# Re-pricing the instructions of a two-block layer for the list schedule that orders them

## The chip, the cores and the metric

The kernel runs on one NeuronCore of one Trainium2 chip. The metric is the device time of one execution in microseconds (us); the slowest core counts, and here there is only one.

## The reference

Two transformer blocks run one after the other on 512 tokens of width 1024, in float32.

```python
def reference(x, ...):
    x = first_block(x, ...)    # hybrid_layer
    return second_block(x, ...)
...
def hybrid_layer(...):
    h = rms_norm(x, norm_pre_w); proj = h @ w_in
    moba_out = moba_attention(a_q, a_k, a_v) * silu(a_z)          # 8 heads of 64
    qkv = silu(causal_depthwise_conv([d_q, d_k, d_v], conv_w))
    o = gated_delta_rule(...)                                     # 4 heads of 128, chunks of 64
    mixed = concat(moba_out, rms_norm(o) * silu(d_z)) @ w_out
    return x + rms_norm(mixed, norm_post_w)
...
def second_block(...):
    y_a = hgrn2_mixer(...)        # 4 heads of 128, gated linear recurrence
    y_b = nsa_mixer(...)          # 8 heads of 64: compressed, selected and window attention
    merged = g_a * (y_a @ w_br_a) + g_b * (y_b @ w_br_b)
    h = x + merged @ w_out
    h = h + square(relu(rmsnorm(h) @ w_ff1)) @ w_ff2
    return rmsnorm(h, final_g)
```

The gated delta rule solves a unit lower triangular system for every head and chunk. HGRN2 masks a product of decayed queries and keys with a causal mask, head by head and tile by tile.

## The kernel before

**An order written by a planner.** The body does not issue instructions. Every call goes to a `Recorder`, which keeps operations with their engine, a price from `cost` in ns and their dependencies from the regions that they read and write. At the end `issue` runs a list schedule: `schedule` simulates five queues (TensorE, VectorE, ScalarE, GpSimd, the DMA issues of SyncE) with these prices, and with a hand-over time between engines from `delay` and the table `HOP`. At each step the engine that is free first takes the ready operation with the best rank. The rank comes from a schedule made backwards from the end, and the forward and backward passes are repeated four times; the order with the shortest planned end is issued. So a price changes no instruction: it changes the place of instructions in the queue of each engine. On the chip each queue runs in that fixed order, and an instruction waits for its inputs there.

All instructions are issued by one line of `issue`, line 274, so every row of the profile shows L274; the tile names tell them apart. `bank` is PSUM, `arena` a large SBUF area of many small tiles, `w_raw`, `w_hi` and `w_lo` weights before and after `split`, `ha`, `hb` and `kr` activations kept as pairs, `sp` small per-row numbers.

**Matrix products.** Each dense product is three TensorE products of split operands: `split` rounds 128x1024 weights on ScalarE (`w_hi`) and takes the rest on VectorE (`w_lo`). A unit is a weight load of 512 KB; two `w_raw` buffers and three of each part are in turn.

**The stages around the change.** The first block mixes, in `ORDER1`, for four delta rule heads `gdn_keys`, `gdn_inverse`, `gdn_states`, `gdn_finish`, the convolutions, and for four pairs of attention heads `moba_proj` and `moba_pair`. `gdn_keys` ends in `block_inverses`: 32 diagonal 16x16 blocks of all chunks lie on 32 partitions, and VectorE multiplies them out there by `tensor_tensor` over 4-dimensional views (4x4x4 and 8x8x8 elements, called block products here) and `tensor_reduce`; ScalarE transposes the result into `XT`, and DMAs carry it through DRAM (`blocks_x`) to the tile that TensorE reads in `gdn_inverse`. `moba_proj` empties PSUM by half partitions: `evq` through `halves`, and `evk`, in 64x512 instructions on ScalarE and VectorE. In the second block `ORDER2` mixes projections, `compress` (adds over `N_CMP` = 31 blocks), `hgrn_gates`, `hgrn_head` (two `copy_predicated` of 64 partitions per tile) and `hgrn_finish`, and then four `nsa_pair` follow. `rstd` and `rstd_of` take a power on GpSimd with `OP.pow`. The rest of the second block is dense products.

Of the kernel before, what the change touches and what calls it, by code (L numbers as in the profile page):

```python
# [30 lines left out]
OP = mybir.AluOpType  # L31
# [12 lines left out]
class Recorder:  # L44
# [5 lines left out]

    ENGINES = ("tensor", "vector", "scalar", "gpsimd", "sync")
    HOP = {("tensor", "vector"): 197, ("tensor", "scalar"): 197, ("tensor", "gpsimd"): 224,
           ("scalar", "scalar"): 148, ("scalar", "vector"): 142, ("scalar", "tensor"): 227,
           ("scalar", "gpsimd"): 170, ("gpsimd", "gpsimd"): 100, ("vector", "vector"): 127, ("vector", "scalar"): 150,
           ("vector", "tensor"): 220, ("vector", "gpsimd"): 155, ("gpsimd", "vector"): 60,
           ("gpsimd", "scalar"): 80, ("gpsimd", "tensor"): 150, ("tensor", "tensor"): 0}
    TABLE = {AF.Exp: 0, AF.Tanh: 0, AF.Ln: 1, AF.Sin: 2}

    def __init__(self, nc):
# [81 lines left out]
    def cost(self, name, method, args, kw):  # L141
        size = lambda a: int(np.prod([x[1] for x in list(a.ap)[1:]])) if len(a.ap) > 1 else 1
        psum = lambda a: isinstance(a, bass.AP) and a.space == PSUM
        n = size(args[0])
        scalars = 61.0 * sum(isinstance(a, bass.AP) for a in args[2:4])
        if method == "dma_start":
            return 475.0
        if name == "tensor":
            if args[1].dtype == F32R:
                return max(n / 2.4 + 13.0, 112.0)  # L150
            if method == "transpose":
                return 110.0
            return max(n / 1.2, 107.0) + max(n, size(args[1])) / 1.2 + 4.0
        if name == "scalar":
            scaled = any(isinstance(kw.get(k), bass.AP) for k in ("scale", "bias"))
            return n / 1.2 + (51.0 if psum(args[1]) else 94.0) + 93.0 * ("accum_out" in kw) + 93.0 * scaled
        if name == "vector":
            if method == "reciprocal":
                return 6.25 * n + 69.0
            if method == "tensor_reduce":  # L160
                n = size(args[1])
            if method == "tensor_tensor_scan":
                n *= 2
            if method == "tensor_tensor":
                return n / 0.96 + 69.0
            if method == "tensor_scalar":
                return n / (0.96 if psum(args[1]) else 1.92) + 69.0 + scalars
            if method == "scalar_tensor_tensor":
                return n / 0.96 + 69.0 + 61.0 * isinstance(args[2], bass.AP)
            two = method == "tensor_copy" and not psum(args[1])  # L170
            return n / (1.92 if two else 0.96) + 67.0
        if method == "tensor_tensor":
            return n * 165.0 + 300.0 if args[3] == OP.pow else n * 2.1 + 100.0
        return n + 70.0

    def transfer(self, out, src):
# [12 lines left out]
    def delay(self, i, k):  # L189

        a, b = self.ops[i], self.ops[k]
        if a.transfer:
            return 100.0
        if a.engine == b.engine and not b.deps[i]:
            return 0.0
        return self.HOP.get((a.engine, b.engine), 100.0)

    def schedule(self, order, before, after):
# [88 lines left out]
N_CMP = 31  # L287
# [1323 lines left out]
```

## Time and profile before

| what | value |
|---|---|
| median of 3 runs | 1114.79 us (1114.76 to 1116.5) |
| profiled execution | 1114.45 us, with a span of 1112.7 us from its first to its last instruction |
| TensorE busy | 1088.8 us, 98% of the span |
| VectorE, ScalarE, GpSimd busy | 781.4, 582.0, 41.1 us |

Busy time of TensorE is made of records whose ends are modelled and which overlap; its idle time is where no record lies. VectorE and ScalarE records also overlap a little with the next one of their queue, so the distance from start to start is shorter than a record where nothing is waited for.

### The profile page before, as it was taken

The numbers are of one execution on the slowest core, as the hardware profiler recorded it, in microseconds if no ns is written. First come the engines' busy times: TensorE is split into PE (matmuls) and PEld (weight loads), VectorE is DVE, ScalarE is ACT, GpSimd is POOL, SyncE is SP. The second block draws the span as 40 slices with busy tenths as digits, with TensorE's granted clock in tenths as the row PEclk, the third lists the DMA queues.
The fourth block names the chain that finished last, engine by engine and source line by source line (L and its number), as shares of the span: only waits on it lengthen the run. The fifth ranks groups of instructions, "written<-read, shape, count | busy, mean of one in ns | idle before, by whom it ended". The sixth has DMA issues, their size and how long they took to land. (4 is left out here: it accounts for less than half of the span.)

```text
span 1112.7 us, 15240 instructions
## 1 busy us (share of the span) xinstructions
PE 1088.8 (98%) x5712; PEld 901.3 (81%) x5712; DVE 781.4 (70%) x1607; ACT 582.0 (52%) x1059; POOL 41.1 (4%) x65
## 2 busy tenths in 40 slices
PE   8999999999999999999999999999999999999997
PEld 7887888787879877888777778888988888888885
DVE  7585877979666446688967654466678578488486
ACT  4655645574455534547765543345553553553564
POOL 1010101001000000000000000000000000000001
PEclk9999999999999999999999999999999999999999
DMA  5323122222542222224201163253205205205102
GB/s 214 133 87 97 50 82 82 79 61 85 177 145 87 102 84 70 67 96 142 96 20 58 44 240 112 96 167 112 102 19 187 97 19 198 105 1 208 38 1 77
DMA packets 44283, 109.60 MB, mean 99 GB/s; under 512 B 10416, under 2 KB 17968, under 8 KB 44208
## 3 DMA queue, kind: packets, MB, share of 16 engines
q1 hardware_dynamic: 44208, 108.62, 28.2%
q8 instruction: 45, 0.74, 0.3%
q14 instruction: 30, 0.25, 0.1%
HBM read 104.67 MB, written 3.93 MB: 98 GB/s over the span
## 5 line engine op out<-in xcount | busy, mean ns | idle before, releaser
L274 PE MATMUL bank<-ha,w_hi 128*128 128x512 f32 (+1 forms) x1504 | 460.7, 384 | 0.0
L274 PEld LDWEIGHTS bank<-ha,w_hi 128*128 128x128 f32 x1504 | 273.0, 189 | 46.2 <-issue 0.8
L274 PE MATMUL bank<-ha,w_lo 128*128 128x512 f32 (+1 forms) x752 | 287.0, 382 | 0.0
L274 DVE TENSOR_TENSOR w_lo<-w_raw,w_hi 128x1024 fp32r<-128x1024 f32 (+2 forms) x106 | 128.0, 1208 | 102.6 <-ACT w_hi L274 101.5
L274 ACT ACTIVATE w_hi<-w_raw 128x1024 fp32r<-128x1024 f32 (+2 forms) x106 | 110.9, 1047 | 153.8 <-PE bank L274 134.2
L274 DVE TENSOR_TENSOR w_lo<-arena,w_hi 128x1024 fp32r<-128x1024 f32 (+2 forms) x94 | 114.0, 1217 | 69.2 <-ACT w_hi L274 68.8
L274 ACT ACTIVATE w_hi<-arena 128x1024 fp32r<-128x1024 f32 (+3 forms) x102 | 102.5, 1005 | 114.9 <-PE bank L274 110.0
L274 PEld LDWEIGHTS bank<-ha,w_lo 128*128 128x128 f32 x752 | 141.8, 189 | 23.2 <-issue 0.3
L274 PE MATMUL bank<-w_hi,hb 128*128 128x512 f32 x416 | 133.6, 393 | 0.3 <-DVE x L274 0.3
L274 ACT ACTIVATE arena<-bank 128x512 f32<-128x512 f32 (+5 forms) x158 | 74.0, 484 | 60.5 <-PE bank L274 57.2
L274 PE MATMUL bank<-w_hi,ha 128*128 128x512 f32 (+3 forms) x384 | 98.1, 343 | 2.1 <-ACT w_hi L274 2.1
L274 ACT ACTIVATE arena<-arena,sp 128x384 f32<-128x384 f32 (+3 forms) x156 | 83.2, 560 | 31.8 <-DVE sp L274 28.0
L274 PE MATMUL bank<-arena 128*128 128x128 f32 (+9 forms) x672 | 96.6, 311 | 1.8 <-DVE arena L274 0.9
L274 PEld LDWEIGHTS bank<-arena 128*128 128x128 f32 (+2 forms) x672 | 76.8, 173 | 21.8 <-issue 12.3
L274 PEld LDWEIGHTS bank<-w_hi,hb 128*128 128x128 f32 x416 | 78.1, 188 | 16.8 <-DVE x L274 0.7
L274 PE MATMUL bank<-ident,arena 128*128 128x128 f32 (+1 forms) x476 | 83.4, 277 | 5.1 <-DVE arena L274 3.4
L274 PE MATMUL bank<-w_lo,hb 128*128 128x512 f32 x208 | 81.6, 392 | 0.4 <-DVE w_lo L274 0.4
L274 PEld LDWEIGHTS bank<-ident,arena 128*128 128x128 f32 (+1 forms) x476 | 58.6, 139 | 25.3 <-DVE arena L274 8.8
L274 PEld LDWEIGHTS bank<-w_hi,ha 128*128 128x128 f32 x384 | 67.0, 191 | 9.8 <-ACT w_hi L274 2.3
L274 PE MATMUL bank<-kr,hb 128*128 128x512 f32 (+3 forms) x288 | 71.3, 352 | 1.9 <-DVE sp L274 1.9
L274 DVE TENSOR_TENSOR arena<-arena 128x1024 f32<-128x1024 f32 (+9 forms) x136 | 69.3, 532 | 3.2 <-ACT arena L274 1.4
L274 POOL TENSOR_TENSOR sp<-sp,mhalf 128x1 f32<-128x1 f32 (+1 forms) x36 | 31.1, 863 | 999.6 <-DVE sp L274 994.9
(161 smaller groups left out, 1371.1 us busy)
## 6 DMA issues: line engine op xcount, KB each, us to landing
w_raw<-in_w_in_dram SPq DMA_DIRECT2D x62, 512.0 KB, 3.3
arena<-in_w_ff_dram SPq DMA_DIRECT2D x43, 512.0 KB, 4.3
w_raw<-in_w_ff_dram SPq DMA_DIRECT2D x21, 512.0 KB, 3.4
w_raw<-in_w_out_dram SPq DMA_DIRECT2D x17, 512.0 KB, 3.4
arena<-in_w_out_dram SPq DMA_DIRECT2D x9, 512.0 KB, 3.5
x<-in_x_dram SPq DMA_DIRECT2D x8, 512.0 KB, 5.6
arena<-in_w_in_dram SPq DMA_DIRECT2D x8, 512.0 KB, 3.2
arena<-blocks_x SPq DMA_DIRECT2D x8, 256.0 KB, 2.9
```

The lines of the kernel that those rows point to most:

```text
L274: self.issued.append((i, getattr(getattr(self.nc, ops[i].engine), method)(*args, **kw)))
```

## The change

The prices of `cost`, the hand-over table and `delay` take other values. No operation is added, removed or resized, and the order of calls in the body stays. All that can differ in the program is the order in which the planner puts them out.

```diff
     HOP = {("tensor", "vector"): 197, ("tensor", "scalar"): 197, ("tensor", "gpsimd"): 224,
-           ("scalar", "scalar"): 148, ("scalar", "vector"): 142, ("scalar", "tensor"): 227,
-           ("scalar", "gpsimd"): 170, ("gpsimd", "gpsimd"): 100, ("vector", "vector"): 127, ("vector", "scalar"): 150,
-           ("vector", "tensor"): 220, ("vector", "gpsimd"): 155, ("gpsimd", "vector"): 60,
-           ("gpsimd", "scalar"): 80, ("gpsimd", "tensor"): 150, ("tensor", "tensor"): 0}
+           ("scalar", "scalar"): 148, ("scalar", "vector"): 142, ("scalar", "tensor"): 250,
+           ("scalar", "gpsimd"): 271, ("gpsimd", "gpsimd"): 100, ("vector", "vector"): 127, ("vector", "scalar"): 150,
+           ("vector", "tensor"): 240, ("vector", "gpsimd"): 165, ("gpsimd", "vector"): 125,
+           ("gpsimd", "scalar"): 118, ("gpsimd", "tensor"): 150, ("tensor", "tensor"): 0}
...
-        n = size(args[0])
+        ap = list(args[0].ap)
+        n, half, small_ = size(args[0]), ap[0][1] == 64, 0.0
+        if name in ("vector", "scalar") and n >= 256 and half and psum(args[1]):
+            small_ = 100.0
+        if name == "vector" and len(ap) > 3 and ap[-1][1] <= 8:
+            small_ += 40.0 + (340.0 if n == 512 else 0.0)
...
-            return n / 1.2 + (51.0 if psum(args[1]) else 94.0) + 93.0 * ("accum_out" in kw) + 93.0 * scaled
+            if ap[0][1] == 32 and len(ap) > 2:
+                small_ = 240.0
+            return small_ + n / 1.2 + (51.0 if psum(args[1]) else 94.0) + 93.0 * ("accum_out" in kw) + 93.0 * scaled
...
             if method == "tensor_tensor":
-                return n / 0.96 + 69.0
+                return small_ + n / 0.96 + 69.0 + (105.0 if ap[-1][1] == N_CMP else 0.0)
+            if method == "copy_predicated":
+                return 302.0
...
             if method == "scalar_tensor_tensor":
-                return n / 0.96 + 69.0 + 61.0 * isinstance(args[2], bass.AP)
+                return small_ + n / 0.96 + 69.0 + 61.0 * isinstance(args[2], bass.AP)
...
         if method == "tensor_tensor":
-            return n * 165.0 + 300.0 if args[3] == OP.pow else n * 2.1 + 100.0
+            return n * 211.0 + 345.0 if args[3] == OP.pow else n * 2.1 + 100.0
...
         if a.engine == b.engine and not b.deps[i]:
-            return 0.0
+            return 0.0 if a.engine == "tensor" else 120.0
```

The last hunk is `delay`: a dependency inside one engine's queue where the later operation overwrites what the earlier one read or wrote, without reading it.

## Rows read from the trace of the kernel before

**Rows 1.** The page's busy time, share of the span and instructions by engine.
```profile
span 1112.7 us, 15240 instructions
PE 1088.8 (98%) x5712; PEld 901.3 (81%) x5712; DVE 781.4 (70%) x1607; ACT 582.0 (52%) x1059; POOL 41.1 (4%) x65
```

**Rows 2.** Windows by stage: length, then busy time by engine, TensorE clock, DMA share.
```profile
0.00:20.00 20.00, 15.20 (x93) 13.94 (x94) 12.67 (x28) 8.84 (x17) 3.42 (x12) 0.91 0.82 298
...
80.00:320.00 240.00, 235.27 (x1353) 192.67 (x1352) 184.07 (x421) 138.67 (x303) 17.42 (x21) 1.00 0.30 98
...
400.00:560.00 160.00, 154.35 (x870) 127.74 (x870) 126.72 (x399) 91.03 (x196) 6.79 (x10) 1.00 0.27 90
...
760.00:1100.00 340.00, 340.00 (x1582) 284.82 (x1581) 245.28 (x301) 169.59 (x213) 3.12 (x4) 1.00 0.24 86
1100.00:1112.70 12.70, 4.68 (x21) 3.52 (x19) 7.56 (x14) 4.12 (x10) 1.10 (x2) 0.79 0.38 143
```

**Rows 3.** Windows of 20 us: a dense one, and the one with most TensorE idle.
```profile
380.00:400.00 20.00, 20.00 (x90) 16.57 (x89) 4.90 (x4) 6.14 (x8) 0.00 (x0) 1.00 0.26 91
...
540.00:560.00 20.00, 18.18 (x117) 14.06 (x116) 19.87 (x76) 17.24 (x51) 0.00 (x0) 1.00 0.15 53
```

**Rows 4.** The waits of TensorE, 80 to 320 us: total, times, longest (us).
```profile
PE bank L274 <- DVE sp L274: 1.9, 2, 1.4
PE bank L274 <- DVE arena L274: 1.7, 4, 0.9
PE bank L274 <- DMA arena<-blocks_x: 0.7, 1, 0.7
```

**Rows 5.** The same for 400 to 560 us.
```profile
PE bank L274 <- DVE arena L274: 3.4, 7, 1.0
```

**Rows 6.** Timeline before the longest wait: start, us, what, [idle before].
```profile
130.85 1.04 DVE L274 TENSOR_TENSOR arena<-arena 32x512 f32<-32x512 f32 x1
...
134.07 1.19 DVE L274 TENSOR_TENSOR arena<-arena 32x512 f32<-32x512 f32 x1
...
137.35 0.50 PE L274 MATMUL bank<-kr,hb 128*128 128x512 f32 x1 [1.42 <-DVE sp L274]
```

**Rows 7.** Timeline, 86 to 204 us: half-partition evacuations back to back.
```profile
88.91 2.40 ACT L274 ACTIVATE kr<-bank 64x512 fp32r<-64x512 f32 x4
...
198.38 2.78 DVE L274 TENSOR_TENSOR kr<-bank,kr 64x512 fp32r<-64x512 f32 x4
```

**Rows 8.** Groups by shape, whole span: count | busy us, mean ns | idle before.
```profile
L274 PE MATMUL bank<-ha,w_lo 128*128 128x512 f32 x656 | 259.8, 396 | 0.0
...
L274 DVE TENSOR_TENSOR x<-x,bank 128x512 f32<-128x512 f32 x72 | 46.2, 678 | 4.7 <-PE bank L274 4.7
...
L274 DVE TENSOR_TENSOR kr<-bank,kr 64x512 fp32r<-64x512 f32 x16 | 11.0, 687 | 1.7 <-ACT kr L274 1.4
...
L274 DVE TENSOR_TENSOR arena<-arena 32x512 f32<-32x512 f32 x8 | 8.7, 1092 | 0.1
...
L274 POOL TENSOR_TENSOR sp<-sp,mhalf 128x4 f32<-128x4 f32 x16 | 19.1, 1192 | 373.3 <-DVE sp L274 373.2
```

**Rows 9.** Timeline, 415 to 437 us: a hand-over to TensorE, a power and its wait.
```profile
416.53 0.42 DVE L274 TENSOR_TENSOR kr<-bank,kr 128x256 fp32r<-128x256 f32 x1
...
417.00 0.44 PE L274 MATMUL bank<-ident,arena 128*128 128x128 f32 x2 [0.71 <-DVE kr L274]
...
433.61 1.92 POOL L274 TENSOR_TENSOR sp<-sp,mhalf 128x4 f32<-128x4 f32 x1 [85.80 <-DVE sp L274]
...
436.40 0.63 PE L274 MATMUL bank<-ident,arena 128*128 128x128 f32 x4 [0.79 <-DVE arena L274]
```

**Rows 10.** Timeline, 494 to 496 us: copies by mask and a wait.
```profile
494.98 0.54 DVE L274 COPY_PREDICATED arena<-hmask,bank 64x128 f32<-64x128 int32 x2
...
495.57 0.33 PE L274 MATMUL bank<-ident,arena 128*128 128x128 f32 x1 [0.40 <-DVE arena L274]
```

**Rows 11.** Timeline at 316 us: a weight split that TensorE waits for.
```profile
316.66 0.51 PE L274 MATMUL bank<-w_lo,hb 128*128 128x512 f32 x1 [0.44 <-DVE w_lo L274]
```

## The prediction

> **What bounds the kernel now.** I read the page's busy shares first. TensorE is busy 1088.8 of 1112.7 us; the next engine, VectorE, 781.4 [rows 1]. The change alters no instruction, so TensorE's work stays, and only its idle 23.9 us can grow or shrink. The second view, the windows by stage, says where that lies [rows 2]: 4.8 us in the first 20 us (loads of the input, and a clock of 0.91 there), 4.7 us between 80 and 320 (the first block's mixers), 5.7 us between 400 and 560 (the second block's), none from 760 to 1100, and 8.0 us in the last window, where TensorE has finished and the last norm and stores run. That leaves 23.9 - 4.8 - 4.7 - 5.7 - 8.0 = 0.7 us elsewhere. So the reorderable part is about 11.1 us in the middle; head and tail are chains of few operations.
>
> Idle time understates a wait. In a dense window TensorE starts 90 products in 20.00 us, one every 0.22 us [rows 3], while the record of one is 0.396 us long [rows 8]. A record thus covers 0.396 - 0.222 = 0.17 us in which nothing new starts, and a wait of 0.4 us costs nearly 0.6.
>
> The third view, TensorE's waits, says what ended them: in 80 to 320 us VectorE's `sp` and `arena` and the landing of `blocks_x`, 1.9 + 1.7 + 0.7 = 4.3 us in 7 waits [rows 4]; in 400 to 560 us VectorE's `arena`, 3.4 us in 7 waits [rows 5]. These are results that came later than the order had counted on.
>
> **The change, price by price.** An operation that the planner thinks too cheap finishes late on the chip, and its consumer then stands at the head of TensorE's queue with other ready products behind it. I compare old and new price with rows. A record of a plain VectorE evacuation is 678 ns [rows 8] and its price 512/0.96 + 69 = 602, so records exceed the time that the queue is held by some 76 ns.
>
> - Block products 32x512: record 1092 less 76 is about 1016; old price 602, new 982. Eight of them, 0.38 each; sixteen small ones get 0.04 each. The transposing ScalarE copy behind them gets 0.24. One head's chain was underpriced by 2 x 0.38 + 4 x 0.04 + 0.24 = 1.16 us. The longest wait of TensorE, 1.42 us, follows two of these products within 7 us [rows 6].
> - Half-partition evacuations: four on VectorE take 2.78 us, (2.78 - 0.687)/3 = 0.698 from start to start; four on ScalarE 2.40 us, about 0.60 [rows 7, 8]. Old prices 602 and 512/1.2 + 51 = 478, new 702 and 578. There are 32 on VectorE and 44 on ScalarE, 0.1 each, and they stand between the block products in the same queue.
> - Copies by mask: two of 64x128 last 0.54 us [rows 10]; the spacing is then about 0.3. Old price 128/0.96 + 67 = 200 (134 for the narrow one), new 302. For a tile's pair that is 0.27 us more. The adds over `N_CMP` blocks in the same stage get 0.105 each, sixteen of them.
> - Powers of four columns: mean record 1192 ns [rows 8]; old 960, new 1189. But one of 1.92 us is among them, and TensorE waited 0.79 us after it [rows 9]. The new price covers 0.23 of the 0.96 us by which that one ran over.
> - Hand-overs. VectorE to TensorE, 220 to 240: the evacuation that starts at 416.53 is priced 336, and TensorE starts at 417.00 [rows 9], 0.13 after its priced end. Both values are longer, the new one by 0.02 more; the order gets a little more slack. GpSimd to its readers gains 0.04 to 0.07. The 120 for overwriting inside one queue has no row that shows it. If the chip takes nothing there, the planner puts another operation into a hole of at most 0.12; if it takes 0.12, the same is saved. I count all hand-overs as nothing, with both signs open, because they work on VectorE and ScalarE, busy 70% and 52% [rows 1].
>
> In all VectorE's prices grow by 8 x 0.38 + 16 x 0.04 + 32 x 0.1 + 16 x 0.27 + 16 x 0.105 = 12.9 us, 1.7% of its work, nearly all of it in the two stages where TensorE waits.
>
> Against the ScalarE half-partition price speaks the Trainium skill, page "Perfetto Trace Analysis", section "Optimizing Scalar/DVE Operations": profiled latency is about twice the overhead that occupies the engine, and that overhead is some 51 ns for ScalarE on PSUM, which by my estimate gives 478, the old price. The spacing of 0.60 in the row disagrees, and the measurement decides; by the page, the new price would be 0.1 us too long for each of the 44, and the gain below would be smaller by at most 0.4 us.
>
> **The sum.** Of the 4.3 us in the first block [rows 4] I take all but 0.3, which stands behind a slow power: 4.0. In the second, four of the seven waits come straight behind copies by mask or those adds, of which [rows 10] shows one; I take a third of 3.4 us, 1.1 [rows 5]. Two slow powers give 2 x 0.23 = 0.5. Ten waits hide 0.17 each, 1.7. Together 7.3 us can be reached by right prices. The planner must find other ready products to fill with, and it moves everything, so new waits appear. Bounds of that share are nothing and all. I take 60%, because the dense windows show that weight products are there to fill with, while in 540 to 560 us VectorE itself is busy 19.87 of 20 us [rows 3] and nothing can be moved off it. That is 4.4 us. The profiled execution of 1114.45 us becomes 1110.1; the median lies 0.34 higher, so 1110.4.
>
> Head and tail I price at nothing. They run one chain: row sums, power, scaling, store. Their small powers go from 465 to 556 but have no other work to trade places with; a swap of two tiles there would cost or save about one 0.7 us operation.
>
> **Rivals.**
> - *The waits only move* (same). The mixers' chains are serial, and TensorE waits at another link. For it: VectorE at 19.87 of 20 us while TensorE idles 1.8 us [rows 3]. Against it: from 80 to 320 VectorE is busy 184 of 240 us [rows 2], so there is room. Time about 1114.
> - *Weight splits come late* (slower). Longer prices on the mixers' chains raise their rank, and the 1024-wide `w_lo` halves drop behind them in VectorE's queue. TensorE already waits 0.44 us for one [rows 11]. Each that slips behind one more 0.69 us operation costs up to 0.69 + 0.17 = 0.86 us. Five slips (4.4/0.86) use the gain up, eight make it slower by over 0.2%; ten, out of 194, give 1110.4 + 8.6 = 1119. Against it: splits run ahead through three buffers.
> - *All of it is recovered* (faster): 7.3 us, and some of the other waits: with all 11.1 us and 0.17 for some twenty waits it would be 14.5. Half of what lies between gives 10.9, so 1104.
> - *The order hardly changes*: prices differ by 1.7% on one engine. Against it: every tie and rank of the list is worked out anew, and a small shift in one queue is passed on. I count it with the first rival.
>
> **How the numbers follow.** Forecast (1106 to 1112.5): 0.48. Full recovery or more: 0.09. No change: 0.22. Slower: 0.21. About 0.2%, 2.2 us, is what a measurement of this kernel can tell from no change. The range reaches from full recovery, 1104, up to the splits' rival near its middle, 1118; that leaves out about 0.07 above and 0.06 below. Faster 0.57, same 0.22, slower 0.21.
>
> **What the next profile should show.** TensorE's records add up to nearly the same work, 5712 products, and its idle time in 80 to 320 us falls from 4.7 to 2 or 3 us; the `blocks_x` wait and the one behind the 32x512 products shorten or vanish; between 400 and 560 the waits behind copies by mask shrink, while those at 540 to 560 stay. Last window and first 20 us stay within 1 us. The prediction is wrong if TensorE's idle time stays at 11 us in the middle with other releasers, if waits for `w_lo` or `w_hi` show up in the dense stretches that had none, or if the head's or tail's chains change by over 1 us.

## The result, and the profile after

The changed kernel took 1104.24 us (median of 4 runs, 1103.69 to 1104.37) against 1115.64 us (4 runs, 1114.76 to 1116.64) for the kernel before: a ratio of 0.9898, 95% interval 0.9886 to 0.991. That is 11.4 us faster. The forecast had the sign and the place, but its 1110.4 us stood for a gain of 4.4, less than half of what came; 1104.24 lies at the very edge of the range. The profiled execution after took 1104.23 us with a span of 1102.5 us, 10.2 less than the span before. The other 1.2 of the 11.4 us lie between the execution profiled before, 1114.45 us, and the median of its kernel; the account below is of the 10.2.

The page after, busy time by engine, to be read against [rows 1] (PE is TensorE and PEld its weight loads, DVE is VectorE, ACT ScalarE, POOL GpSimd; every row now shows L283, the line of `issue` in the changed kernel):

```profile
span 1102.5 us, 15240 instructions
PE 1086.6 (99%) x5712; PEld 901.8 (82%) x5712; DVE 779.2 (71%) x1607; ACT 581.5 (53%) x1059; POOL 40.0 (4%) x65
```

The counts of each engine are the same to the last instruction; only the order differs. The span less TensorE's busy time is 1102.5 - 1086.6 = 15.9 us, where it was 23.9. The windows by stage after (columns as in [rows 2]; the last is GB/s):

```profile
80.00:320.00 240.00, 239.13 (x1382) 197.16 (x1381) 188.82 (x428) 140.75 (x306) 18.67 (x22) 1.00 0.32 100
...
400.00:560.00 160.00, 157.66 (x903) 130.46 (x901) 128.50 (x421) 95.41 (x210) 5.74 (x10) 1.00 0.26 87
560.00:740.00 180.00, 179.84 (x909) 141.93 (x908) 103.85 (x235) 83.98 (x166) 0.00 (x0) 1.00 0.32 110
```

TensorE's idle time falls from 4.73 to 240 - 239.13 = 0.87 us in the first block's mixers and from 5.65 to 2.34 in the second's. In the stage behind them it grows from nothing to 0.16. The first 20 us (4.80 and 4.82) and 740 to 760 (0.74) are as they were. The window from TensorE's last record to the end, before and after, in this order:

```profile
1104.68:1112.70 8.02, 0.00 (x0) 0.00 (x0) 2.88 (x6) 2.24 (x6) 1.10 (x2) 0.67 0.35 131
```

```profile
1095.49:1102.50 7.01, 0.00 (x0) 0.00 (x0) 2.27 (x4) 2.06 (x4) 0.79 (x2) 0.69 0.40 151
```

So the 10.2 us are 3.9 in the first mixers, 3.3 less 0.2 in the second, 1.0 in the tail, and 1088.8 - 1086.6 = 2.2 inside TensorE's records. I read these 2.2 as pauses which the records cover, as the prediction did; no view shows such a pause by itself.

What TensorE still waits for, in 80 to 320 us and then in 400 to 560 us (against [rows 4, 5] and, of the kernel before, one more row of 400 to 560 us):

```profile
PE bank L274 <- DVE kr L274: 1.0, 2, 0.7
```

```profile
PE bank L283 <- ACT hb L283: 0.5, 1, 0.5
PE bank L283 <- DMA arena<-blocks_x: 0.4, 1, 0.4
```

```profile
PE bank L283 <- ACT w_hi L283: 0.6, 2, 0.3
PE bank L283 <- ACT arena L283: 0.5, 2, 0.3
PE bank L283 <- DVE w_lo L283: 0.5, 1, 0.5
PE bank L283 <- DVE sp L283: 0.3, 1, 0.3
PE bank L283 <- DVE arena L283: 0.2, 1, 0.2
```

The first list has lost its waits for VectorE, the 6 of [rows 4] and the one of [rows 11], and has one of 0.5 us for ScalarE's `hb` that is new; `blocks_x` is down from 0.7 to 0.4. In the second VectorE's `arena` went from 3.4 us in 7 waits to 0.2 in one, the 1.0 us for `kr` are gone, and weight parts come up as new, smaller releasers. No wait of a TensorE product in the changed kernel is put down to a copy by mask; before, three were, 1.0 us in all. The timeline shows how it came about in the second block product chain, the one of [rows 6] (start, us, what):

```profile
130.32 0.56 DVE L283 CUSTOM_DVE_ANT_0 arena<-bank,sq 128x384 f32<-128x384 f32 x1
...
131.07 0.55 DVE L283 CUSTOM_DVE_ANT_0 arena<-bank,sq 128x384 f32<-128x384 f32 x1
...
134.92 1.03 DVE L283 TENSOR_TENSOR arena<-arena 32x512 f32<-32x512 f32 x1
...
137.07 1.12 DVE L283 TENSOR_TENSOR arena<-arena 32x512 f32<-32x512 f32 x1
```

The kernel before had the two rows of the same kind and size behind both of its products, the first of them here, and TensorE started at 137.35 [rows 6], just after its end:

```profile
136.75 0.54 DVE L274 CUSTOM_DVE_ANT_0 arena<-bank,sq 128x384 f32<-128x384 f32 x1
```

The `CUSTOM_DVE` rows are the softmax's pass over a PSUM bank, which reads the scores and so frees the bank for the next product; the waiting product reads nothing of its result. The block products last about as long as they did (1.04 and 1.19 us before), but these passes now stand ahead of them in VectorE's queue, and in 80 to 320 us no wait for `sp` is left.

The stretch that I had called full, the first attention pairs of the second block at 540 to 560 us [rows 3], lies at 520 to 540 us now:

```profile
520.00:540.00 20.00, 19.65 (x112) 15.69 (x111) 19.12 (x70) 16.80 (x46) 0.00 (x0) 1.00 0.28 102
540.00:560.00 20.00, 19.48 (x115) 12.56 (x113) 14.77 (x60) 13.94 (x40) 0.00 (x0) 1.00 0.05 21
```

VectorE is nearly as full, 19.12 of 20 us, yet TensorE's idle time there is 0.35 us where it was 1.82. Counted over the 30 us that hold the same attention pairs, 530 to 560 before and 520 to 550 after, it is 0.74 us where it was 1.97. Most of the waiting before came behind weight splits (start, us, what); two rows of before and one of after:

```profile
543.21 1.22 DVE L274 TENSOR_TENSOR w_lo<-arena,w_hi 128x1024 fp32r<-128x1024 f32 x1
...
545.08 0.55 PE L274 MATMUL bank<-ident,arena 128*128 128x128 f32 x3 [0.99 <-DVE arena L274]
```

```profile
530.33 1.22 DVE L283 TENSOR_TENSOR w_lo<-arena,w_hi 128x1024 fp32r<-128x1024 f32 x1
```

Before, this split and another at 547.16 each stood right ahead of a copy of attention weights out of PSUM, and TensorE waited 0.99 and 0.51 us until those two copies were done, 1.5 of the 1.82 us. After, the first of the two comes four softmax passes earlier in VectorE's queue; the second has kept its place, and TensorE no longer waits there, for a reason that is not shown.

### The profile page after: what moved, and what is told of

It reads as the page before. It is cut to its first block, busy times and chain, and to the rows that moved or that the text cites. A ratio compares the mean times of both kernels' runs of the same rounds, so it can differ in the third digit from the quotient of the medians.

```text
span 1102.5 us, 15240 instructions
## 1 busy us (share of the span) xinstructions
PE 1086.6 (99%) x5712; PEld 901.8 (82%) x5712; DVE 779.2 (71%) x1607; ACT 581.5 (53%) x1059; POOL 40.0 (4%) x65
## 4 chain that ended last, share of the span: by engine, by line
PE 88%; DVE 7%; DMA 3%; ACT 1%; issue 1%; POOL 0%; POOLq 0%; SPq 0%; ACTq 0%; DVEq 0%
PE bank L283 88%; DVE arena L283 3%; DVE w_lo L283 1%; DMA w_raw<-in_w_out_dram 1%; ACT w_hi L283 1%; DMA arena<-in_w_out_dram 1%; DVE x L283 1%; DMA arena<-in_norm_pre_w_dram 0%; DVE kr L283 0%; DMA blocks_x<-arena 0%; DVE sp L283 0%; DMA arena<-blocks_x 0%; DVE sq L283 0%; ACT arena L283 0%; POOL sp L283 0%
## 5 line engine op out<-in xcount | busy, mean ns | idle before, releaser
L283 PE MATMUL bank<-ha,w_hi 128*128 128x512 f32 (+1 forms) x1504 | 460.3, 384 | 0.2 <-ACT w_hi L283 0.2
L283 PEld LDWEIGHTS bank<-ha,w_hi 128*128 128x128 f32 x1504 | 273.0, 189 | 46.5 <-issue 1.2
L283 PE MATMUL bank<-ha,w_lo 128*128 128x512 f32 (+1 forms) x752 | 287.4, 383 | 0.0
L283 ACT ACTIVATE w_hi<-w_raw 128x1024 fp32r<-128x1024 f32 (+2 forms) x106 | 111.1, 1049 | 161.0 <-PE bank L283 143.4
L283 DVE TENSOR_TENSOR w_lo<-w_raw,w_hi 128x1024 fp32r<-128x1024 f32 (+2 forms) x106 | 127.9, 1208 | 95.4 <-ACT w_hi L283 91.7
L283 ACT ACTIVATE w_hi<-arena 128x1024 fp32r<-128x1024 f32 (+3 forms) x102 | 102.5, 1006 | 117.7 <-PE bank L283 106.6
L283 DVE TENSOR_TENSOR w_lo<-arena,w_hi 128x1024 fp32r<-128x1024 f32 (+2 forms) x94 | 114.1, 1217 | 69.0 <-ACT w_hi L283 68.6
L283 PEld LDWEIGHTS bank<-ha,w_lo 128*128 128x128 f32 x752 | 141.8, 189 | 23.6 <-issue 0.4
L283 PE MATMUL bank<-w_hi,hb 128*128 128x512 f32 x416 | 132.6, 392 | 0.3 <-DVE x L283 0.3
L283 ACT ACTIVATE arena<-bank 128x512 f32<-128x512 f32 (+5 forms) x158 | 74.6, 482 | 60.4 <-PE bank L283 57.5
L283 PE MATMUL bank<-w_hi,ha 128*128 128x512 f32 (+3 forms) x384 | 99.6, 345 | 2.1 <-ACT w_hi L283 2.1
L283 ACT ACTIVATE arena<-arena,sp 128x128 f32<-128x128 f32 (+3 forms) x156 | 83.7, 568 | 28.4 <-DVE sp L283 25.8
L283 PE MATMUL bank<-arena 128*128 128x128 f32 (+9 forms) x672 | 97.2, 311 | 0.6 <-DMA arena<-blocks_x 0.4
L283 PEld LDWEIGHTS bank<-arena 128*128 128x128 f32 (+2 forms) x672 | 77.3, 173 | 20.5 <-issue 11.8
L283 PEld LDWEIGHTS bank<-w_hi,hb 128*128 128x128 f32 x416 | 78.0, 188 | 16.4 <-DVE x L283 0.7
L283 PE MATMUL bank<-ident,arena 128*128 128x128 f32 (+1 forms) x476 | 82.3, 275 | 0.8 <-ACT arena L283 0.5
L283 PE MATMUL bank<-w_lo,hb 128*128 128x512 f32 x208 | 81.6, 393 | 0.0
L283 PEld LDWEIGHTS bank<-w_hi,ha 128*128 128x128 f32 x384 | 67.6, 192 | 9.8 <-ACT w_hi L283 2.3
L283 PEld LDWEIGHTS bank<-ident,arena 128*128 128x128 f32 (+1 forms) x476 | 59.1, 140 | 18.9 <-DVE arena L283 3.7
L283 PE MATMUL bank<-kr,hb 128*128 128x512 f32 (+3 forms) x288 | 71.9, 355 | 0.3 <-DVE sp L283 0.3
L283 DVE TENSOR_TENSOR arena<-arena 128x1024 f32<-128x1024 f32 (+9 forms) x136 | 68.2, 531 | 2.6 <-ACT arena L283 1.4
L283 PE MATMUL bank<-w_lo,ha 128*128 128x512 f32 (+3 forms) x192 | 65.9, 345 | 0.5 <-DVE w_lo L283 0.5
```

What stands on the lines that cost most here:

```text
L283: self.issued.append((i, getattr(getattr(self.nc, ops[i].engine), method)(*args, **kw)))
```

## The experiments

Sixteen kernels, each a different set of prices for the same program; none leaves out or adds work. Ratios are to executions of the kernel before that were taken beside each (medians 1115.40 to 1116.14 us), so they compare across rows better than the medians do. Idle is TensorE's in 80 to 320 and in 400 to 560 us, from the same windows of one profiled execution each.

| kernel | median us | ratio, 95% interval | idle, us |
|---|---|---|---|
| before | 1115.64 | 1 | 4.73, 5.65 |
| changed | 1104.24 | 0.9898 (0.9886 to 0.991) | 0.87, 2.34 |
| e1_prices | 1105.82 | 0.9921 (0.9904 to 0.9939) | 0.92, 3.16 |
| e1_hands | 1111.24 | 0.9962 (0.9947 to 0.9977) | 3.63, 4.66 |
| e1_chain | 1110.44 | 0.9955 (0.994 to 0.9971) | 0.10, 4.97 |
| e1_mask | 1114.1 | 0.9986 (0.9977 to 0.9996) | 5.70, 3.77 |
| e2_jit_after_a | 1106.5 | 0.992 (0.9905 to 0.9934) | 1.44, 1.97 |
| e2_jit_after_b | 1105.09 | 0.9907 (0.9892 to 0.9921) | 1.12, 2.77 |
| e2_jit_before_a | 1115.86 | 1.0005 (0.9996 to 1.0014) | 3.94, 5.50 |
| e2_jit_before_b | 1111.52 | 0.9969 (0.9956 to 0.9981) | 2.79, 3.58 |
| e3_reversed | 1122.0 | 1.0062 (1.0047 to 1.0077) | 8.33, 6.54 |
| e3_hop | 1114.11 | 0.9986 (0.9976 to 0.9995) | 2.56, 5.88 |
| e3_delay | 1113.43 | 0.9981 (0.9972 to 0.9991) | 2.90, 5.14 |
| e3_even | 1114.05 | 0.9993 (0.9983 to 1.0002) | 3.37, 4.94 |
| e4_jit_prices_a | 1106.19 | 0.991 (0.9895 to 0.9925) | 0.69, 2.62 |
| e4_jit_prices_b | 1108.83 | 0.9937 (0.992 to 0.9953) | 1.55, 4.18 |
| e4_jit_hands_a | 1113.66 | 0.998 (0.9971 to 0.9989) | 4.67, 4.97 |
| e4_jit_hands_b | 1113.23 | 0.9972 (0.9961 to 0.9983) | 3.50, 5.10 |

**Which part does it.** Theory A says that right prices remove waits where they were wrong; B, that the order of before was a bad draw and any other order a new one; C, that longer hand-overs give slack. B allows nearly any time for a single order, so only several orders together can speak against it. The first four kernels take one part each.

`e1_prices` is the changed kernel with the hand-overs of before:

```diff
-           ("vector", "tensor"): 240, ("vector", "gpsimd"): 165, ("gpsimd", "vector"): 125,
+           ("vector", "tensor"): 220, ("vector", "gpsimd"): 155, ("gpsimd", "vector"): 60,
...
-            return 0.0 if a.engine == "tensor" else 120.0
+            return 0.0
```

> All prices of operations as in the changed kernel, the hand-over table and the 120 for overwriting inside one queue as before. Theory A (right prices remove the waits): nearly the whole gain, 1104 to 1107 us against 1115.6. Theory B (the order of before was an unlucky draw, and any other order is a new draw): anywhere from 1104 to 1116. Theory C (longer hand-overs give the order slack): at most 3 us of the gain, 1112 to 1116.

`e1_hands` is the reverse, the kernel before with the new hand-over table and `delay`:

```diff
-           ("vector", "tensor"): 220, ("vector", "gpsimd"): 155, ("gpsimd", "vector"): 60,
+           ("vector", "tensor"): 240, ("vector", "gpsimd"): 165, ("gpsimd", "vector"): 125,
...
-            return 0.0
+            return 0.0 if a.engine == "tensor" else 120.0
```

> Only the hand-over table and the 120 for overwriting inside one queue, prices as before. Theory A: within 2 us of before, 1113 to 1117. Theory B: anywhere from 1104 to 1118. Theory C: most of the gain, 1105 to 1109.

`e1_chain` is the kernel before with, of the new prices, only `small_`:

```diff
+        if name in ("vector", "scalar") and n >= 256 and half and psum(args[1]):
+            small_ = 100.0
+        if name == "vector" and len(ap) > 3 and ap[-1][1] <= 8:
+            small_ += 40.0 + (340.0 if n == 512 else 0.0)
...
+            if ap[0][1] == 32 and len(ap) > 2:
+                small_ = 240.0
```

> Only the prices of block products, of half-partition evacuations and of the transposing ScalarE copy; copies by mask, adds, powers and hand-overs as before. Theory A: TensorE's idle time from 80 to 320 us falls from 4.7 to about 1.5 us while 400 to 560 us keeps 4 to 6; 1109 to 1112 us. Theory B: both stages change, in either direction. Theory C: within 2 us of before.

`e1_mask` is the kernel before with only the others:

```diff
-                return n / 0.96 + 69.0
+                return small_ + n / 0.96 + 69.0 + (105.0 if ap[-1][1] == N_CMP else 0.0)
+            if method == "copy_predicated":
+                return 302.0
...
-            return n * 165.0 + 300.0 if args[3] == OP.pow else n * 2.1 + 100.0
+            return n * 211.0 + 345.0 if args[3] == OP.pow else n * 2.1 + 100.0
```

with `small_` always 0.

> Only the prices of copies by mask, of the adds over compressed blocks and of powers. Theory A: TensorE's idle time from 400 to 560 us falls from 5.7 to about 3 us while 80 to 320 us keeps 4 to 5; 1111 to 1114 us. Theory B: both stages change, in either direction. Theory C: within 2 us of before.

The prices alone give 0.79% of the 1.02%, inside A's range. The chain's prices take the first stage to an idle time of 0.10 us and leave the second nearly alone, as A said. The first window of `e1_chain`:

```profile
80.00:320.00 240.00, 239.90 (x1384) 198.18 (x1383) 187.16 (x427) 141.95 (x306) 17.08 (x22) 1.00 0.31 99
```

`e1_mask` lowers the second stage from 5.65 to 3.77, not as far as A's 3, and its first stage goes up to 5.70, over A's 4 to 5; its time is 0.1 us above A's range. That both stages changed and the time stayed within 2 us of before is what B and C had said of this kernel. The two parts alone give 0.45 and 0.14%, less together than the 0.79% of both. `e1_hands` gave 4.3 us (1111.24 against 1115.55 for the kernel before beside it), which fits neither A (within 2 us) nor C (most of the gain); B allows it.

**A draw of the order?** Three kernels shake the prices: every VectorE and ScalarE price is multiplied by a number between 0.983 and 1.017 that depends on the operation's place in the list.

```diff
-        op.cost += self.cost(name, method, args, kw)
+        price = self.cost(name, method, args, kw)
+        if name in ("vector", "scalar"):
+            price *= 1.0 + 0.017 * (2.0 * ((i * 7919 + 101) % 1009) / 1008.0 - 1.0)
+        op.cost += price
```

Set b has 577 in the place of 101. `e3_reversed` is the kernel before with the surcharges of the new prices subtracted, as far as a price stays positive:

```diff
+            small_ = -100.0
...
+            small_ -= 40.0 + (340.0 if n == 512 else 0.0)
...
+                small_ = -240.0
...
+                return small_ + n / 0.96 + 69.0 - (105.0 if ap[-1][1] == N_CMP else 0.0)
+            if method == "copy_predicated":
+                return 98.0 if n == 128 else 30.0
...
+            return n * 119.0 + 255.0 if args[3] == OP.pow else n * 2.1 + 100.0
```

> The changed kernel with every VectorE and ScalarE price altered at random by up to 1.7% either way. Theory A: right prices stay right within that, so 1103 to 1108 us. Theory B: the good order is lost, 1104 to 1116, likely over 1108.

> The kernel before with every VectorE and ScalarE price altered at random by up to 1.7% either way. Theory A: the wrong prices stay wrong, 1112 to 1118 us. Theory B: a new draw, likely faster than 1112.

> The same as the run before it with other random numbers. Theory A: 1112 to 1118 us. Theory B: a new draw, likely faster than 1112, and some us away from the first.

> The prices of before with the new surcharges subtracted in place of added (32x512 products 222, half-partition 502 and 378, copies by mask 98 and 30, powers 255 + 119 per column), hand-overs as before. Theory A: the errors double and the waits grow, 1119 to 1128 us. Theory B: any draw, 1104 to 1118.

The shaken kernels of before took 1115.86 and 1111.52: the second is 0.5 under A's range and as B had it, so a draw of some 4 us exists. The shaken changed kernel stayed at 1106.5. The reversed prices gave 1122.0, the slowest of all, as A said and B did not; it is one order, and was not shaken. Its waits of TensorE in 80 to 320 us, at the same releasers as in [rows 4] but 7.7 us of them where there were 3.6:

```profile
PE bank L283 <- DVE sp L283: 5.0, 4, 1.8
PE bank L283 <- DVE arena L283: 2.7, 5, 1.8
```

**Slack, and the two halves of the hand-overs.** Three changes to the kernel before: `e3_hop` has only the new table, `e3_delay` only the 120, and `e3_even` spreads 1.7% over all of VectorE, here in this order:

```diff
-           ("vector", "tensor"): 220, ("vector", "gpsimd"): 155, ("gpsimd", "vector"): 60,
+           ("vector", "tensor"): 240, ("vector", "gpsimd"): 165, ("gpsimd", "vector"): 125,
```

```diff
-            return 0.0
+            return 0.0 if a.engine == "tensor" else 120.0
```

```diff
-        op.cost += self.cost(name, method, args, kw)
+        op.cost += self.cost(name, method, args, kw) * (1.017 if name == "vector" else 1.0)
```

> Only the hand-over table, all else as before. It splits the 4.3 us that table and overwriting gave together. Slack theory (longer hand-overs to TensorE and from GpSimd put consumers later): 1111 to 1113 us, with fewer waits in both mixer stages. Draw theory: a change of this size without a cause, since small random prices alone gave 1111.5 and 1115.9: 1111 to 1117.

> Only the 120 for overwriting inside one queue. If the chip really takes it: 1111 to 1113 us, as the pair did. If it takes nothing there: 1114 to 1118. Draw theory: 1111 to 1117.

> Every VectorE price of before times 1.017, the same 1.7% that the change adds in all, spread evenly. If mere slack on VectorE were the cause: 1105 to 1109 us. If the prices must stand at the right operations: 1112 to 1117.

> The changed kernel with other random alterations of up to 1.7%. Right prices: 1103 to 1109 us, all below the two altered kernels of before (1111.5, 1115.9). Draw theory: one of them above 1110.

Even slack of the same total gives nothing that can be told from no change (0.9993, interval 0.9983 to 1.0002), and its time lies in the range for prices that must stand at the right operations, far above the 1105 to 1109 of mere slack. So slack spread over VectorE does not explain the gain. It is one order, and its idle time in the two stages, 8.31 us, is below the 10.38 of before, as a new draw may be. The table alone and the 120 alone gave 0.14% and 0.19%, together less than the 0.38% of both; the table's 1114.11 missed its slack range, 1111 to 1113, and the 1113.43 of the 120 lies between its two, 1111 to 1113 and 1114 to 1118, so it decides nothing. Both lie in the range of a draw, 1111 to 1117. The changed kernel shaken with set b stayed at 1105.09.

**Hand-overs, in pairs.** The last four complete a table of old and new prices, old and new hand-overs, each unshaken and with sets a and b. `e4_jit_prices_*` is `e1_prices` shaken, `e4_jit_hands_*` is `e1_hands` shaken.

> New prices, old hand-overs, with the first set of random alterations. If the hand-overs give 1.5 to 4 us on their own, this stays 1.5 to 4 us above the altered changed kernel of the same set (1106.5): 1108 to 1111. If their share was the draw: within 1.5 of it in either direction.

> The same with the second set, whose changed kernel took 1105.1. Hand-overs give something: 1106.6 to 1109. Draw: 1103.6 to 1106.6.

> Old prices, new hand-overs, first set; the altered kernel of before took 1115.9. Hand-overs give something: 1111.5 to 1114. Draw: 1114.4 to 1118, or anything with no pattern over the sets.

> The same with the second set, whose kernel of before took 1111.5. Hand-overs give something: 1107 to 1110. Draw: 1110 to 1116.

Of these four, `e4_jit_prices_b` and `e4_jit_hands_a` came out as if the hand-overs gave something, `e4_jit_prices_a` and `e4_jit_hands_b` as if they gave nothing.

| ratio to before | unshaken | set a | set b |
|---|---|---|---|
| old prices, old hand-overs | 1 | 1.0005 | 0.9969 |
| old prices, new hand-overs | 0.9962 | 0.998 | 0.9972 |
| new prices, old hand-overs | 0.9921 | 0.991 | 0.9937 |
| new prices, new hand-overs | 0.9898 | 0.992 | 0.9907 |

New against old prices, down a column: -0.79, -0.95 and -0.32 points with the old hand-overs, -0.64, -0.60 and -0.65 with the new. All six go one way, on average -0.66 points or 7.3 us. New against old hand-overs: -0.38, -0.25, +0.03 and -0.23, +0.10, -0.30, four one way and two the other, on average -0.17 points or 1.9 us, which six such pairs do not tell from a draw. The six kernels with new prices have 0.69 to 1.55 us idle in the first stage, the six with old prices 2.79 to 4.73.

What these kernels do not separate is a right price from one that is merely higher at the same operations: none has surcharges larger than the new ones. Nor was any of the new prices tried by itself.

## Why the prediction was right in kind and wrong in size

**Right.** TensorE's work stayed and its waits shrank; the two mixer stages are where 7.0 of the 10.2 us came from; the prices of the operations named were the cause. That is shown by six pairs of orders that all go one way; reversed prices added waits, and the same total spread evenly gave nothing that can be told from no change. That the new prices worked because they are right, and not only higher, is argued from the rows and was not tried.

The price checks stand in the main: block products, half-partition evacuations and copies by mask last after the change as they did. For the half-partition evacuations on ScalarE the record alone would not show it: 590 ns for 64x512 in both profiles, and 595 for a full-partition 128x512 that is priced 478. The spacing shows it. Two full-partition ones take 1.06 us together (at 8.69 us of the kernel before), so they start some 0.47 apart, where half-partition ones start 0.60 apart [rows 7]. One reading was wrong: the pair of [rows 10] is not two copies of 64x128 but one of 64x128 and one of 64x64, as `hgrn_head` issues them and the counts (16 each) say. The wide one then takes 0.54 - 0.23 = 0.31 us to the start of the next, near its 302 ns; the narrow one, with a record of 234 ns, went from 134 to the same 302, which no row supports.

**Wrong: "I take 60%", and in the second stage the reach that it multiplied.** I expected 60% of 7.3 us, that is 3.4 of visible idle time and 1.0 covered by records. Measured were 7.0 us of visible idle time in the middle (11.1 to 4.1) and 2.2 inside records, more than the whole of the 7.3. The two stages went wrong differently.

In the first the reach was right and the share was not: of the 4.0 us that I took as reachable 3.9 went. `e1_chain` even removed 4.63 of 4.73 us, with the 0.3 behind a slow power and the wait for a weight part that I had left out of reach. So there the fill was not a matter of six tenths: an order with right prices finds ready products for nearly every wait.

In the second the reach was too small: I had counted a third of the 3.4 us [rows 5], 1.1 us straight behind copies by mask and adds, besides the slow powers, and nothing of the 1.0 us for `kr`; 3.3 of 5.65 us went. Waits behind rightly priced operations went too.

The reason that I gave for the 60% fell too. I took VectorE's 19.87 of 20 us [rows 3] for a limit that no order could lift, and expected the waits there to stay. The row of 520 to 540 us after the change has 19.12 of 20 and a fifth of the idle time. A queue can be full and TensorE still not wait: for the longest wait there, 0.99 us, it mattered which of VectorE's operations came first, the split of 1.22 us or the copy that TensorE waited for.

**Wrong: "I count all hand-overs as nothing".** On average they are worth 1.9 us in six pairs, two of which go the other way. That is less than what set b alone does to the kernel before, 0.31 points. How much of the surplus is theirs stays open, and so does whether the 120 matches the chip: no row shows that delay, and `e3_delay` fell between its two ranges.

**Wrong: head and tail at nothing.** The head was right. The tail shortened by 1.0 us, just at the 1 us that I had named as a sign of being wrong. TensorE's last record ends at 1104.68 before and 1095.49 after, and the last addition that reads its sums (start, us, what) starts here, before and then after:

```profile
1105.22 0.68 DVE L274 TENSOR_TENSOR x<-x,bank 128x512 f32<-128x512 f32 x1
```

```profile
1095.53 0.69 DVE L283 TENSOR_TENSOR x<-x,bank 128x512 f32<-128x512 f32 x1 [0.42 <-PE bank L283]
```

Before, it started 0.54 us behind TensorE, held up in VectorE's queue by two multiplications with the final weight and a sum for the next norm; after, VectorE had been idle for 0.42 us and starts it 0.04 us behind TensorE. That is half of the 1.0; the other half comes in the step from that addition to the next such sum, 2.11 us before (1105.22 to 1107.33) and 1.60 after (1095.53 to 1097.13): a scaling on ScalarE stands in the way of the square between them, which starts 0.69 us behind the addition's end before and 0.17 after.

**The rivals.** "The waits only move" is refuted here: idle time fell in sum and not by place alone, in the two stages together to 3.2 to 5.7 us in the six kernels with new prices, against 6.4 to 10.4 in the six with old. "Weight splits come late" did turn up, as 0.6 + 0.5 us for `w_hi` and `w_lo` in 400 to 560 us, where there had been none. That is one of the signs that I had named for being wrong, at a tenth of the gain and not more. "All of it is recovered" with its 1104 came closest in size, at 10.9 us forecast against 11.4, though I gave it 0.09 and not all was recovered: visible waits 7.0, covered ones 2.2, tail 1.0, and 4.1 us of idle time left in the middle. The forecast for 80 to 320 us, 2 or 3 us of idle time, was beaten by 0.87.

## What to carry to other kernels

In a program whose order comes from a planner, compare each price with the distance from start to start of that operation in the trace, and correct it at the operations that are slow; the same total spread evenly bought nothing here that could be told from no change. If the bottleneck engine has independent work to fill with, do not count only the waits straight behind wrongly priced operations as removable: here 82% of the idle time of one stage and 59% of the other went, waits behind rightly priced operations among them. Before crediting a change of an order with a few tenths of a per cent, shake the prices a little and see how far the time moves by itself: here up to 0.3%.

## What the runs showed that I had not expected

- Random prices within 1.7% moved the kernel before between 1111.52 and 1115.86 us, while the changed one moved only between 1104.24 and 1106.5. That right prices make the order less sensitive is not shown by this: the other two rows of the table moved by 2.4 us with old prices (1111.24 to 1113.66) and by 3.0 with new ones (1105.82 to 1108.83).
- The records of TensorE, for the same 5712 products, cover 1086.6 us in the changed kernel and 1088.8 in the one before. So its busy time is not a fixed amount of work here; it shrank by 2.2 us together with the waits.
